# A row gather with three direct batches instead of five, a first index group of two, and slots dealt from another table

## The chip, the cores and the metric

The kernel runs on one core of a Trainium2 chip. The metric is the device time of one execution in microseconds (us); the median over several executions is compared. The engines of the core run side by side, each through its own list of instructions in order: TensorE (PE, with PEld for its weight loads), VectorE (DVE), ScalarE (ACT), GpSimd (POOL) and SyncE (SP). Transfers between memory and the chip run on sixteen DMA engines that all queues share.

## The reference

There are 32 batches. Each has a table of 512 rows with 1024 float32 values, and 128 row numbers; the output of a batch is the rows that the numbers name, in their order.

```python
batch, seq, dim = 32, 512, 1024
x = np.random.randn(batch, seq, dim).astype(np.float32)
indices = np.random.randint(0, seq, (batch, 128)).astype(np.int32)
...
for b in range(batch):
    result[b] = x[b, indices[b]]
```

Row numbers repeat within a batch. In the inputs of this case a batch names between 110 and 120 different rows, so about one row in nine or ten would be read twice by a plain gather. All 4096 output rows of 4 KB (16.8 MB) have to be written.

## The kernel before, in words

**Direct batches.** The first `HEAD` = 5 batches are gathered plainly: GpSimd issues an indirect DMA of 128 rows into a block (line 144, through `gather`, line 121), and SyncE stores the block (`store`, line 137). They need only the row numbers as a column, which `idxT` (line 112) holds after one transpose on TensorE; batch 0 has its column from a small load of its own.

**Packed batches.** The other 27 batches read each different row once. They stand in groups of three (`GROUP`), and for each group the index work has three steps. `step0` (line 166) spreads the row numbers of each batch over all partitions (`bc`, by TensorE), counts for every position how many earlier positions name the same row (`junk`, `cnt`, on VectorE), and marks the first of each kind as its leader (`lead`); `past` adds up the leaders of earlier batches. `step1` (line 183) numbers the leaders (`rk`, `nth`), and compares these numbers with the table `turn` (line 92), which says for each of the 128 slots which number it takes (`pack`). `step2` (line 196) puts the leader's row number into its slot (`pos`, `at`), with a value over the limit in the empty ones, and makes the matrix `s` that says which output row is served by which slot. `fetch` (line 207) issues the indirect DMA into one of `RING` = 8 buffers `u`; a slot with a value over the limit moves nothing. `spread_rows` (line 238) multiplies `s` with the buffer on TensorE (two halves of 512 columns), ScalarE copies the result from PSUM into the block, and SyncE stores it.

A number runs on from batch to batch (through `past`, taken modulo 128), so the empty slots of the next batch begin where those of the last one ended. `turn` comes from `rank`, eight GpSimd iotas (lines 73 to 79).

**The half batch.** Batch `HALF` = `HEAD` is served in two ways. Its rows below 256 are loaded plainly and early by ScalarE's queue (`early`, line 101) and spread by `half_rows` (line 225) with `last` false, four TensorE instructions for each half of the columns; only its rows from 256 on are gathered. `half_spread` (line 217) makes the matrix `same` for this on VectorE.

**Order.** TensorE, VectorE and ScalarE's first instructions run in the order in which the program names them (`InOrder`, line 13); GpSimd and SyncE too. Ahead of the main loop four groups (`AHEAD`) are prepared (lines 249 to 262). As buffers are eight, gathers up to batch `HEAD + RING - 1` = 12 are issued there. In this stretch `half_rows` for the first half stands after group 1's steps, and for the second half after group 2's. The main loop (line 263) takes the batches in turn: spread it, store it, fetch the batch eight further on into the buffer that came free, and do one of the three steps for the group four further on.

PSUM holds two buffers of `bc` (line 58), so that of a group is written anew two groups later, after all its readers.

Of the kernel before, what the change touches and what calls it, by code (L numbers as in the profile page):

```python
# [6 lines left out]
F32 = mybir.dt.float32  # L7
# [21 lines left out]
def kernel(ctx, tc, x, indices, out):  # L29
# [11 lines left out]

    nc = tc.nc
    B, S, D = x.shape
    N = indices.shape[1]
    HEAD, RING, GROUP, AHEAD, FAR = 5, 8, 3, 4, 1024
    HALF = HEAD
    PAIRED = range(12, 20)
    GROUPS = (B - HEAD) // GROUP  # L50
    assert 2 * N <= S <= FAR and (B - HEAD) % GROUP == 0
    const = ctx.enter_context(tc.tile_pool(name="const", bufs=1))
    ring = ctx.enter_context(tc.tile_pool(name="ring", bufs=1))
    rows = ctx.enter_context(tc.tile_pool(name="rows", bufs=1))
# [15 lines left out]

    diff = const.tile([N, N], I32, name="diff")
    nc.gpsimd.iota(diff[:], pattern=[[1, N]], base=0, channel_multiplier=-1)
    rank = const.tile([N, 8, 16], I32, name="rank")
    for e in range(8):
        fold = 0
        for bit, col in enumerate((6, 5, 3)):
            fold ^= col * (e >> bit & 1)
        steps = [[(-16 if fold >> bit & 1 else 16) << bit, 2] for bit in (2, 1, 0)]
        nc.gpsimd.iota(rank[:, e], pattern=[[1, 2]] + steps, base=2 * e + 16 * fold, channel_multiplier=0)
    less = const.tile([N, 1], F32, name="less")  # L80
    zero = const.tile([N, 1], F32, name="zero")
    dve(v.memset, zero[:], 0.0)
# [6 lines left out]
    dve(v.tensor_copy, out=less[:], in_=diff[:, 0:1])  # L89
    every = const.tile([N, N], F16, name="every")  # L90
    dve(v.memset, every[:], 1.0)
    turn = const.tile([N, N], F16, name="turn")
    dve(v.tensor_copy, out=turn[:], in_=rank[:].rearrange("p e q -> p (e q)"))
    vf = const.tile([N, N], F16, name="vf")
    dve(v.memset, vf[:], 0.0)
    dve(v.tensor_copy, out=vf[:B],
        in_=vals[:].bitcast(I32).rearrange("p (n two) -> p n two", two=2)[:, :, 0])


    xf = x.flatten_outer_dims()  # L100
# [49 lines left out]

    cnt, lead, slot = table("cnt", F32), table("lead", F16), table("slot", F16)
    nth, at = table("nth", I32), table("at", I32)
    past = const.tile([N, B + 1], F16, name="past")
    dve(v.memset, past[:, HEAD:HEAD + 1], 0.0)
    bcs, packs, spread = {}, {}, {}

    def of_group(g):
        return range(HEAD + g * GROUP, HEAD + (g + 1) * GROUP)

    def cols(t, g):  # L160
        return t[:, HEAD + g * GROUP:HEAD + (g + 1) * GROUP]

    def wide(t):
        return t.rearrange("p (g o) -> p g o", o=1).to_broadcast([N, GROUP, N])

    def step0(g):

        bcs[g] = bc = pbc.tile([N, 4, N], F32, name="bc")
        for k, b in enumerate(of_group(g)):
            pe(mm, bc[:, k], lhsT=ident[:, b:b + 1].to_broadcast([N, N]), rhs=vf[:], start=True, stop=True)  # L170
        for k, b in enumerate(of_group(g)):
            junk = junkp.tile([N, N], F16, name="junk")
            dve(v.scalar_tensor_tensor, out=junk[:], in0=bc[:, k], scalar=idxF[:, b:b + 1], in1=below[:],
                op0=ALU.is_equal, op1=ALU.mult, accum_out=cnt[:, b:b + 1])
        if HALF in of_group(g):
            c = slice(HALF, HALF + 1)
            dve(v.scalar_tensor_tensor, out=cnt[:, c], in0=idxF[:, c], scalar=2.0 * N, in1=cnt[:, c],
                op0=ALU.is_lt, op1=ALU.add)
        dve(v.tensor_scalar, out=cols(lead, g), in0=cols(cnt, g), scalar1=0.0, scalar2=None, op0=ALU.is_equal)
        for b in of_group(g):  # L180
            dve(v.tensor_tensor, out=past[:, b + 1:b + 2], in0=past[:, b:b + 1], in1=lead[:, b:b + 1], op=ALU.add)

    def step1(g):

        rk = psm.tile([N, GROUP], F32, name="rk")
        pe(mm, rk[:], lhsT=above[:], rhs=cols(lead, g), start=True, stop=False)
        pe(mm, rk[:], lhsT=every[:], rhs=cols(past, g), start=False, stop=True)
        dve(v.tensor_copy, out=cols(nth, g), in_=rk[:])
        dve(v.tensor_scalar, out=cols(nth, g), in0=cols(nth, g), scalar1=N - 1, scalar2=None, op0=ALU.bitwise_and)
        dve(v.scalar_tensor_tensor, out=cols(slot, g), in0=cols(cnt, g), scalar=256.0, in1=cols(nth, g),  # L190
            op0=ALU.mult, op1=ALU.add)
        packs[g] = pack = junkp.tile([N, GROUP, N], F16, name="pack")
        dve(v.tensor_tensor, out=pack[:], in0=turn[:].rearrange("p (o n) -> p o n", o=1).to_broadcast([N, GROUP, N]),
            in1=wide(cols(slot, g)), op=ALU.is_equal)

    def step2(g):

        pos = psm.tile([N, GROUP], F32, name="pos")
        for k, b in enumerate(of_group(g)):
            pe(mm, pos[:, k:k + 1], lhsT=packs[g][:, k], rhs=near[:, b:b + 1], start=True, stop=True)  # L200
        dve(v.tensor_scalar, out=cols(at, g), in0=pos[:], scalar1=float(FAR), scalar2=None, op0=ALU.add)
        s = pick.tile([N, GROUP, N], F32, name=f"s{g}")
        dve(v.tensor_tensor, out=s[:], in0=bcs[g][:, :GROUP], in1=wide(cols(at, g)), op=ALU.is_equal)
        for k, b in enumerate(of_group(g)):
            spread[b] = s[:, k]

    def fetch(b):
        if HEAD <= b < B:
            gather(held[(b - HEAD) % RING][:], at[:, b:b + 1], b, bounds_check=S - 1, oob_is_err=False)
# [7 lines left out]
    def half_spread():  # L217

        same = pick.tile([N, 2, N], F32, name="same")
        for k in range(2):  # L220
            dve(v.tensor_scalar, out=same[:, k], in0=bcs[0][:, HALF - HEAD], scalar1=less[:], scalar2=float(k * N),
                op0=ALU.add, op1=ALU.is_equal)
        spread[HALF, "early"] = [same[:, k] for k in range(2)]

    def half_rows(h, last):
        w = slice(h * 512, (h + 1) * 512)
        if not last:
            spread[HALF, h] = pout.tile([N, 512], F32, name="ps")
        ps = spread[HALF, h]
        if last:  # L230
            pe(mm, ps[:], lhsT=spread[HALF], rhs=held[(HALF - HEAD) % RING][:, w], start=False, stop=True)
        else:
            for k in range(2):
                pe(mm, ps[:], lhsT=spread[HALF, "early"][k], rhs=early[k][:, w], start=k == 0, stop=False)
        if last:
            nc.scalar.copy(out=blocks[HALF][:, w], in_=ps[:])  # L236
# [10 lines left out]
        store(b)  # L247

    step0(0)
    step0(1)  # L250
    for g in range(AHEAD):
        step1(g)
        if 0 < g < AHEAD - 1:
            step0(g + 1)
        step2(g)
        for b in of_group(g):
            if b < HEAD + RING:
                fetch(b)
        if g == 0:
            half_spread()  # L260
        elif g < 3:
            half_rows(g - 1, False)
    for b in range(HEAD, B):
        spread_rows(b)
        fetch(b + RING)
        g, step = divmod(b - HEAD, GROUP)
        if g + AHEAD < GROUPS:
            (step0, step1, step2)[step](g + AHEAD)


# [28 lines left out]
```

## Time and profile before

| | us |
|---|---|
| median of 9 runs | 88.13 |
| range of the runs | 87.92 to 89.08 |
| the profiled execution, its own time | 88.75 |
| its span, first to last instruction | 87.0 |

| engine | busy us | share of the span |
|---|---|---|
| TensorE | 62.2 | 72% |
| ScalarE | 40.6 | 47% |
| GpSimd | 33.5 | 39% |
| VectorE | 31.6 | 36% |

The transfers of the profiled execution are 32.91 MB, 379 GB/s over the span. The queue q1 carries the stores and the loads of the row numbers (SyncE), q0 the gathers (GpSimd), q10 the two early loads (ScalarE).

How to read the lines of a profile: in the order of time a line has its start in us, how long it took (for merged instructions: from the first start to the last end, or their sum), the engine, the line of the program, the operation, the tiles written and read, and the number of instructions; in brackets stands how long the engine was idle before and what ended that. "issue" is idle time for which the trace shows no wait. A line number can be that of a helper: the instructions that go through `InOrder` show line 21 or 24, those of both gathers line 122.

### The profile page before, as it was taken

What the parts mean: (1) busy time and instruction counts of PE and PEld (TensorE: products, weight loads), DVE (VectorE), ACT (ScalarE), POOL (GpSimd) and SP (SyncE); (2) the same over time, 40 slices, a digit from 0 to 9 for tenths busy, and PEclk for the clock granted to TensorE, in tenths of its full rate; (3) what the DMA queues carried; (4) which work ended last, traced back from release to release, by engine and by line L of the source; (5) the groups of instructions that cost most, each with busy time, mean ns of one, the idle gap of its engine ahead of it and who ended that gap; (6) DMA issues with size and microseconds to landing.
All of it is one profiled execution on the core that took longest, in us unless ns stands there. A gap on an engine that the chain in (4) does not pass through costs nothing.

```text
span 87.0 us, 829 instructions
## 1 busy us (share of the span) xinstructions
PE 62.2 (72%) x189; PEld 25.5 (29%) x189; DVE 31.6 (36%) x160; ACT 40.6 (47%) x63; POOL 33.5 (39%) x45
## 2 busy tenths in 40 slices
PE   0040169596799999999999988778878888785000
PEld 0030133241344444443544443222333333221000
DVE  3289895582565386473754850000000000000000
ACT  0999910000165665566566555553454454555000
POOL 7557577738044455554445554333400000000000
PEclk9999999999999999999999999999999999999955
DMA  0898999999999999999999999999999999999950
GB/s 1 279 403 237 290 317 394 416 411 416 420 418 420 420 416 420 420 416 409 420 420 420 413 418 418 422 422 415 420 415 415 420 418 422 418 422 420 420 243 11
DMA packets 9637, 32.91 MB, mean 379 GB/s; under 512 B 1585, under 2 KB 1617, under 8 KB 9633
## 3 DMA queue, kind: packets, MB, share of 16 engines
q1 hardware_dynamic: 4736, 16.81, 47.5%
q0 software_dynamic: 4608, 15.01, 44.6%
q10 hardware_dynamic: 288, 1.05, 3.2%
q8 instruction: 1, 0.02, 0.1%
q14 instruction: 4, 0.02, 0.1%
HBM read 17.86 MB, written 16.78 MB: 398 GB/s over the span
## 4 chain that ended last, share of the span: by engine, by line
DMA 37%; PE 30%; DVE 11%; issue 11%; POOL 2%; ACT 1%; SPq 0%; POOLq 0%; DVEq 0%
DMA u<-in_x_dram,at 34%; PE ps L24 27%; DMA vals<-in_indices_dram 3%; DVE pack L24 3%; DVE junk L24 2%; DVE nth L24 2%; POOL u L122 2%; DVE past L24 1%; PE pos L24 1%; DVE slot L24 1%; ACT block L246 1%; DVE s L24 1%; DVE same L24 1%; PE bc L24 1%; SPq L66 0%
## 5 line engine op out<-in xcount | busy, mean ns | idle before, releaser
L24 PE MATMUL ps<-u,s 128*128 128x512 f32 x108 | 52.0, 610 | 5.0 <-DMA u<-in_x_dram,at 5.0
L122 POOL DMA_INDIRECT u<-in_x_dram,at x27 | 26.9, 997 | 25.3 <-PE bc L24 6.3
L246 ACT COPY block<-ps 128x512 f32<-128x512 f32 x36 | 21.1, 586 | 18.8 <-PE ps L24 17.8
L24 PEld LDWEIGHTS ps<-u,s 128*128 128x128 f32 x108 | 18.3, 189 | 26.8 <-ACT block L246 15.0
L246 ACT COPY pair<-ps 128x512 f32<-128x512 f32 x16 | 9.4, 586 | 5.8 <-PE ps L24 4.2
L24 DVE SCALAR_TENSOR_TENSOR junk<-bc,idxF,below 128x128 f16<-128x128 f32 x27 | 8.0, 348 | 6.2 <-PE bc L24 6.2
L24 ACT COPY u<-zero 128x1024 f32<-128x1024 f32 x8 | 7.7, 1038 | 0.0
L24 PE MATMUL ps<-early,same 128*128 128x512 f32 x8 | 7.5, 1092 | 0.0
L236 ACT COPY block<-ps 128x512 f32<-128x512 f32 x2 | 1.2, 586 | 12.7 <-PE ps L24 12.7
L24 PE MATMUL pos<-near,pack 128*128 128x1 f16 x27 | 2.0, 167 | 5.5 <-DVE pack L24 5.5
L24 DVE TENSOR_TENSOR pack<-turn,slot 128x384 f16<-128x384 f16 x9 | 5.0, 558 | 0.3
L24 DVE TENSOR_TENSOR s<-bc,at 128x384 f32<-128x384 f32 x9 | 5.0, 558 | 0.3
L24 DVE TENSOR_TENSOR past<-past,lead 128x1 f16<-128x1 f16 x27 | 4.4, 163 | 0.9
L122 POOL DMA_INDIRECT block<-in_x_dram,idxT x4 | 3.8, 947 | 2.0 <-DVE past L24 1.0
L24 PEld LDWEIGHTS <-pack 128*128 128x128 f16 x27 | 1.7, 100 | 9.5 <-DVE pack L24 8.0
L24 PE MATMUL bc<-vf,ident 128*128 128x128 f16 x27 | 3.4, 256 | 1.3 <-DVE same L24 1.3
L24 PEld LDWEIGHTS <-ident 128*128 128x128 f16 x27 | 2.4, 112 | 4.2 <-issue 4.2
L21 PE MATMUL pos<-ident,vf 128*128 128x32 f16 x1 | 0.2, 209 | 4.2 <-DVE vf L24 4.2
L24 PEld LDWEIGHTS ps<-early,same 128*128 128x128 f32 x8 | 2.4, 324 | 2.1 <-issue 2.1
L24 DVE TENSOR_SCALAR at<-pos 128x3 int32<-128x3 f32 x9 | 1.4, 160 | 4.2 <-PE pos L24 3.8
L24 DVE CAST nth<-rk 128x3 int32<-128x3 f32 x9 | 1.4, 160 | 4.2 <-PE rk L24 3.5
L24 ACT ACT_TABLE_LOAD x1 | 1.3, 1283 | 2.2 <-DVE ident L24 2.2
(31 smaller groups left out, 18.0 us busy)
## 6 DMA issues: line engine op xcount, KB each, us to landing
out_dram<-block SPq DMA_DIRECT2D x24, 512.0 KB, 8.3
out_dram<-pair SPq DMA_DIRECT2D x4, 1024.0 KB, 12.5
early<-in_x_dram ACTq DMA_DIRECT2D x2, 512.0 KB, 4.2
u<-in_x_dram,at POOLq DMA_INDIRECT x27, 11.6
block<-in_x_dram,idxT POOLq DMA_INDIRECT x4, 7.0
vals<-in_indices_dram SPq DMA_DIRECT2D x1, 32.0 KB, 2.7
first<-in_indices_dram SPq DMA_DIRECT2D x1, 1.0 KB, 1.8
block<-in_x_dram,first POOLq DMA_INDIRECT x1, 5.0
```

The lines of the kernel that those rows point to most:

```text
L21: self.last = do(*args, **kw)
L24: self.last = do(*args, **kw)
L122: nc.gpsimd.indirect_dma_start(out=dst, out_offset=None, in_=xf[:], in_offset=bass.IndirectOffsetOnAxis(ap=at, axis=0), element_offset=b * ...
L236: nc.scalar.copy(out=blocks[HALF][:, w], in_=ps[:])
L246: nc.scalar.copy(out=blocks[b][:, w], in_=ps[:])
```

## The change

- `HEAD` is 3 instead of 5: batches 3 and 4 are packed, 29 in all, and the half batch is 3. The eight buffers now take batches 3 to 10 ahead of the loop.
- The groups are lists: the first has two batches (3 and 4), the nine others three.
- The steps are cut into smaller functions. `step0` is `spread_indices` (TensorE) and `find_leads` (VectorE); `step2` is `fill_slots` (to `at`) and `match` (`s`). In the stretch ahead of the loop, the next group's `spread_indices` stands before `fill_slots`, its `find_leads` after it, and `match` last. `half_spread` moves from the end of group 0 to a place behind `step1` of group 1, and the two calls of `half_rows` come one group later: after `fill_slots` of groups 2 and 3.
- Numbers in a group come from accumulated matmuls (`earlier`): each batch adds the leaders of the batches before it in its group; `past` is kept once a group, in `count_on`, behind `match`.
- The table `turn` has two parts. The first deals sixteen consecutive numbers to the slot groups (4 slots each) in another order; group 0 reads it from PSUM, where a matmul spreads it. The second part is for the last two batches (`APART`), which start from number 0 each; it puts their last numbers, which stay empty, into slots 38, 39, 42, 43, 46, 47, 50, 51, 71 to 76 and 104.
- The cast of `turn` on VectorE moves behind that of `vf`.
- In the main loop each group of batches does the three steps for the group four further on; the first group has two batches, so two of the steps stand after its second batch.

```diff
-    HEAD, RING, GROUP, AHEAD, FAR = 5, 8, 3, 4, 1024
+    HEAD, RING, GROUP, AHEAD, FAR = 3, 8, 3, 4, 1024
...
-    GROUPS = (B - HEAD) // GROUP
+    APART = B - 2
+    groups = [range(HEAD, HEAD + 2), *(range(b, b + GROUP) for b in range(HEAD + 2, B, GROUP))]
...
-    rank = const.tile([N, 8, 16], I32, name="rank")
-    for e in range(8):
-        fold = 0
-        for bit, col in enumerate((6, 5, 3)):
-            fold ^= col * (e >> bit & 1)
-        steps = [[(-16 if fold >> bit & 1 else 16) << bit, 2] for bit in (2, 1, 0)]
-        nc.gpsimd.iota(rank[:, e], pattern=[[1, 2]] + steps, base=2 * e + 16 * fold, channel_multiplier=0)
+    rank = const.tile([N, 2, N], I32, name="rank")
+    nc.gpsimd.iota(rank[:, 0], pattern=[[8, 2], [64, 2], [1, 8], [16, 4]], base=0, channel_multiplier=0)
+    for p0, p1, at0 in ((0, 38, 0), (52, 71, 44), (77, 104, 63), (105, N, 90), (71, 77, 121), (104, 105, 127)):
+        nc.gpsimd.iota(rank[:, 1, p0:p1], pattern=[[1, p1 - p0]], base=at0, channel_multiplier=0)
+    twos = rank[:, 1, 38:54].rearrange("p (k a l) -> p k a l", a=2, l=2)
+    nc.gpsimd.iota(twos[:, :3, 1], pattern=[[2, 3], [1, 2]], base=38, channel_multiplier=0)
+    nc.gpsimd.iota(twos[:, :, 0], pattern=[[2, 4], [1, 2]], base=113, channel_multiplier=0)
...
-    turn = const.tile([N, N], F16, name="turn")
-    dve(v.tensor_copy, out=turn[:], in_=rank[:].rearrange("p e q -> p (e q)"))
...
+    turn = const.tile([N, 2, N], F16, name="turn")
+    dve(v.tensor_copy, out=turn[:], in_=rank[:])
...
+        if g == 0:
+            pe(mm, bc[:, GROUP], lhsT=ident[:, 0:1].to_broadcast([N, N]), rhs=turn[:, 0], start=True, stop=True)
...
     def step1(g):
 
         rk = psm.tile([N, GROUP], F32, name="rk")
-        pe(mm, rk[:], lhsT=above[:], rhs=cols(lead, g), start=True, stop=False)
-        pe(mm, rk[:], lhsT=every[:], rhs=cols(past, g), start=False, stop=True)
-        dve(v.tensor_copy, out=cols(nth, g), in_=rk[:])
+        n, like = len(groups[g]), dealt_on(g)
+        earlier = [(k, lead[:, groups[g][0]:groups[g][0] + like - k]) for k in range(1, like)]
+        if g:
+            earlier.append((0, past[:, g:g + 1].to_broadcast([N, like])))
+        pe(mm, rk[:, :n], lhsT=above[:], rhs=cols(lead, g), start=True, stop=not earlier)
+        for i, (k, more) in enumerate(earlier):
+            pe(mm, rk[:, k:like], lhsT=every[:], rhs=more, start=False, stop=i == len(earlier) - 1)
+        dve(v.tensor_copy, out=cols(nth, g), in_=rk[:, :n])
...
+        table = turn[:, 0:1] if g else bcs[0][:, GROUP:]
+        dve(v.tensor_tensor, out=pack[:, :like], in0=table.to_broadcast([N, like, N]),
+            in1=wide(cols(slot, g)[:, :like], like), op=ALU.is_equal)
+        if like < n:
+            dve(v.tensor_tensor, out=pack[:, like:], in0=turn[:, 1:2].to_broadcast([N, n - like, N]),
+                in1=wide(cols(slot, g)[:, like:], n - like), op=ALU.is_equal)
...
     step0(0)
-    step0(1)
     for g in range(AHEAD):
         step1(g)
-        if 0 < g < AHEAD - 1:
-            step0(g + 1)
-        step2(g)
-        for b in of_group(g):
+        if g == 1:
+            half_spread()
+        if g < AHEAD - 1:
+            spread_indices(g + 1)
+        fill_slots(g)
+        for b in groups[g]:
             if b < HEAD + RING:
                 fetch(b)
-        if g == 0:
-            half_spread()
-        elif g < 3:
-            half_rows(g - 1, False)
-    for b in range(HEAD, B):
-        spread_rows(b)
-        fetch(b + RING)
-        g, step = divmod(b - HEAD, GROUP)
-        if g + AHEAD < GROUPS:
-            (step0, step1, step2)[step](g + AHEAD)
+        if g > 1:
+            half_rows(g - 2, False)
+        if g < AHEAD - 1:
+            find_leads(g + 1)
+        match(g)
+    for g, batches in enumerate(groups):
+        steps = [(step0, g + AHEAD), (step1, g + AHEAD), (step2, g + AHEAD)]
+        for b in batches:
+            spread_rows(b)
+            fetch(b + RING)
+            for step, ahead in steps if b == batches[-1] else steps[:1]:
+                if ahead < len(groups):
+                    step(ahead)
+            steps = steps[1:]
```

## The prediction

> **What bounds the kernel now.** I read the page first, part 2 and part 3.
>
> ```profile
> DMA  0898999999999999999999999999999999999950
> GB/s 1 279 403 237 290 317 394 416 411 416 420 418 420 420 416 420 420 416 409 420 420 420 413 418 418 422 422 415 420 415 415 420 418 422 418 422 420 420 243 11
> DMA packets 9637, 32.91 MB, mean 379 GB/s; under 512 B 1585, under 2 KB 1617, under 8 KB 9633
> ...
> q1 hardware_dynamic: 4736, 16.81, 47.5%
> q0 software_dynamic: 4608, 15.01, 44.6%
> ```
>
> A slice is 2.17 us. From slice 7 (15 us) to slice 37 the transfer engines run at 409 to 422 GB/s: 32.91 MB set the end, and what counts is whether the transfer queues ever run empty. The busy times by stage confirm the rate (columns: stretch, length, then busy us of PE, PEld, DVE, ACT, POOL, the clock, DMA share, GB/s).
>
> ```profile
> 24.00:28.00 4.00, 4.00 (x14) 1.72 (x13) 2.62 (x14) 2.53 (x5) 1.99 (x2) 1.00 1.03 417
> 28.00:84.00 56.00, 46.52 (x132) 18.43 (x130) 14.06 (x66) 28.72 (x49) 16.94 (x17) 0.99 1.02 417
> ```
>
> Next, the DMA view cut at 24 us and at 28 us (one line of each) says how much had been moved, and the view of 24 to 28 us what moved then.
>
> ```profile
> DMA packets 2437, 7.83 MB, mean 326 GB/s; under 512 B 502, under 2 KB 534, under 8 KB 2436
> ...
> DMA packets 2952, 9.50 MB, mean 339 GB/s; under 512 B 610, under 2 KB 642, under 8 KB 2951
> ...
> q0 software_dynamic: 486, 1.60, 98.6%
> q1 hardware_dynamic: 29, 0.07, 4.2%
> ```
>
> Between 24 and 28 us almost only gathers (q0) run: the early stores are used up and the first spread block isn't stored yet. The backlog of gathers, built before the main loop, keeps the engines busy there. Last, the order of time shows when that loop starts.
>
> ```profile
> 2.77 1.12 POOL L122 DMA_INDIRECT block<-in_x_dram,first  x1 [0.46 <-DMA first<-in_indices_dram]
> ...
> 8.69 0.94 POOL L122 DMA_INDIRECT block<-in_x_dram,idxT  x1 [0.30 <-issue]
> ...
> 9.64 0.16 DVE L24 TENSOR_SCALAR at<-pos 128x3 int32<-128x3 f32 x1 [0.34 <-PE rk L24]
> ...
> 10.59 1.00 POOL L122 DMA_INDIRECT u<-in_x_dram,at  x1 [0.96 <-ACT u L24]
> ...
> 12.13 3.76 PE L24 MATMUL ps<-early,same 128*128 128x512 f32 x4
> ...
> 17.32 3.73 PE L24 MATMUL ps<-early,same 128*128 128x512 f32 x4
> ...
> 20.90 0.99 POOL L122 DMA_INDIRECT u<-in_x_dram,at  x1 [0.30 <-issue]
> ...
> 22.45 1.96 PE L24 MATMUL ps<-u,s 128*128 128x512 f32 x4
> ...
> 24.69 1.00 POOL L122 DMA_INDIRECT u<-in_x_dram,at  x1 [2.80 <-PE bc L24]
> ```
>
> The gather at 20.90 is the eighth and last that the ring's eight buffers allow. The ninth waits until TensorE has read the first buffer: the loop starts at 22.45 and that gather goes out at 24.69.
>
> **The margin before.** What is queued ahead of the loop: early rows 1.05 MB, five direct gathers plus eight packed ones (640 + 864 rows of 4 KB, counting the distinct indices of the inputs) 6.16 MB, five stores 2.62 MB; together 9.83 MB. With 9.50 MB moved by 28 us it lasts to 28.8. The gather of 24.69 has its first packet some 2.3 us later (the first gather, issued at 2.77, has its first packet record at 5.08), at 27.0. So the engines stay fed by 1.8 us.
>
> **What the skill says.** "DMA: Bandwidth & Descriptors", section Issuing engines are not separate DMA queues: transfers of ScalarE, SyncE and GpSimd share the same sixteen engines and interleave. The trace agrees: q0 and q1 together stay at 417 GB/s whichever leads. The same page, The descriptor swizzle: the engine of partition p is 8*(p>>6) + ((p>>2)&7). No view names an engine; the count below rests on this. "TensorE: Matmul & The Clock Gate", Part 1: a cold array runs at half clock until a free-running window of about 3.4 us was busy throughout. The trace agrees: the fp32 matmuls of the 12.13 and 17.32 rows start 0.85 us apart, those of 22.45 0.43 us; the change came at 20.9 us.
>
> **The change, part by part.**
>
> *Two direct batches become packed (HEAD 5 to 3).* Removed: two direct gathers of 128 rows, 0.94 us and a 0.30 us gap each on POOL. Added: two packed ones (56 rows for the half batch 3, 111 for batch 4), two pairs of spread matmuls (1.9 us each), four copies (0.59 each). By count 3664 gathered rows become 3632: 0.13 MB less, 0.3 us at 417 GB/s. The matmuls and copies lie under the transfers of the loop (46.5 of 56 us are PE's there). But the queue ahead of the loop shrinks: early 1.05, gathers 384 + 852 rows 5.06, three stores 1.57: 7.68 MB instead of 9.83. Before moved 7.83 MB by 24 us, so this is gone at 23.7, and the ninth gather would have to be issued by 21.4.
>
> *When does the loop start?* Followed by rows of before.
> - Iotas on POOL: eight of 16 elements took 1.26 us; nine now, the largest 128 elements (like diff, 0.22): about 1.45. They end near 2.5; the gather waits to 2.77 for its indices anyway. Cost 0 to 0.1; past the cover it would delay the first gather one for one.
> - The cast of turn (256 columns, about 0.36 by the 128-column row's 0.23) moves behind vf, 4.15 to 4.5; TensorE's transpose lies beside it until 4.44. Cost 0 to 0.05.
> - Group 0 (batches 3, 4): two junk instead of three saves 0.27; no second step0 and no past chain ahead of nth save 2.2 (before, lead ended at 6.05 and nth began at 8.15). nth 6.0, then 0.2 each to slot, pack of 256 elements from PSUM 0.43 (a new form: 384 fp16 took 0.56, 384 fp32 from PSUM 0.56, so 0.35 to 0.56), pos 0.25, at done near 7.45 (before 9.80). The gather followed at by 0.79; so 8.25. POOL would be free at 7.44.
> - Group 1: three junk and lead 1.1, s of two 0.43, past 0.35, nth to pack 1.2 to 10.7, same 0.55 (half_spread now stands ahead of fill_slots), then bc of group 2, which waits for same (before too: PE bc <- DVE same 1.3), pos, at near 12.0; gathers 12.8, 14.1, 15.4.
> - Group 2: junk to lead 1.1, s 0.56, past 0.6, nth to pack 1.2, hops 0.5: pos near 15.6; gathers 16.8, 18.1, 19.4. The last is batch 10, as 3 + 8 is 11.
> - Half rows: the first pair begins at 15.7 and holds TensorE 3.6 us cold (12.10 to 15.68 before). Group 3's rk, queued behind it, runs at 19.35; nth to pos takes 1.55 (15.7 to 17.2 before): 20.9. Only then the second pair, 3.6: **loop at 24.5, not 22.45.** Before, both pairs were over when group 3's chain ended; here the second comes after it, and batch 3's matmuls are queued behind.
> - Batch 3: 1.8 us warm, 3.6 cold. TensorE works without a break from 20.9; a busy window ends between 24.3 and 27.7. I take 2.6: 27.1. The ninth gather (0.44 later, as 24.25 to 24.69) goes at 27.5, its packets at 29.8. The store (0.8 later, as 24.25 to 25.07) goes at 27.9, its packets 1.0 to 2.5 later (a load on idle engines 1.0, store 0 2.5, from the packet records). **Transfers resume at about 29.2: idle for 5.5 us**, bounds 4.3 to 6.7.
>
> *Rest.* 32.78 - 7.68 = 25.1 MB at 417 GB/s are 60.2 us: 89.4. For before the same sum gives 28.0 + 23.41/0.417 = 84.1; the landing records of the last store have a mean of 84.37.
>
> *The first group's steps in the loop.* Step1 and step2 of group 4 both follow batch 4, so pos waits on TensorE for pack, 1.5 us, with batch 5's matmuls behind. The two batches before it supply 30.7 rows per engine, 4.8 us; batch 5 is done 5.5 us after batch 3. Cost 0 to 0.7; taken 0.5: 89.9. Later groups have one step per batch as now.
>
> *Dealing.* By the map both dealings give each engine the same total (229 rows each before; 227 after, if the last two batches were dealt alike). In the landing records of before's last store the engines end at 83.38 to 86.05: three stand out, 1.68, 1.07 and 0.56 beyond the mean. With the last two batches apart, engine 10 gets 219 rows, 2 to 4 get 225, engine 1 and 9 and 11 227, the others 228 or 229. At 0.157 us a row (65536 B at 417 GB/s) engine 10 is 1.26 us below the mean, the others at most 0.31 above. If the late engines are those, the last ends 0.75 beyond the mean: 0.9 gained. If not, up to 0.3 lost. Taken: 90.65.
>
> *The other edits* (count_on behind s, no past memset, accumulating matmuls of 0.03 to 0.17) are in the chains above; in the loop they hide under transfers, and cost 0.2 a group where that cover is gone.
>
> **Sum.** 90.65 and the 0.95 after the last landing (86.05 to 87.0): span 91.6, 4.6 over before. The profiled execution took 88.75, 0.62 over the median of 88.13; I put the difference on the median: **92.7 us**.
>
> **Rivals.**
> 1. *The gap is shorter (0.12).* TensorE is warm by the second half pair. It then takes 1.8 instead of 3.6 and batch 3 1.8: resuming at 26.8, 2.4 sooner, 90.3 us. For it: one window's phase decides. Against: before, the first pair did not warm the array.
> 2. *The gap and no relief (0.14).* The late engines are others than the table's: 0.9 lost again and 0.3 more, 93.9 us. The view can't tell.
> 3. *No gap, faster (0.05).* If the ninth gather is out by 21.4 us, the queues never empty; then only 0.3 (rows) and 0.9 (dealing) remain: 86.9 us. For it: group 0 is ready 2.3 us sooner. Against: two cold half pairs and group 3's chain fill 15.7 to 24.5 on TensorE.
> 4. *Nothing moves (0.02)*: a small gap of about 1 us against the dealing, 88.1.
>
> My forecast has 0.67, its own range 91.5 to 93.7. **Numbers.** The 8-in-10 range takes the cases of rivals 1 and 2 in part: 90.5 to 94.2. Under 0.5% this kernel's runs can't be told from no change; slower 0.93, same 0.02, faster 0.05.
>
> **What would show it.** Right: GB/s falls to near zero in slices 11 to 13, q0 and q1 both; the eighth packed gather is issued near 19.4 and the ninth near 27.5; the first "ps<-u,s" stands near 24.5, after the second "ps<-early,same"; at least 0.12 MB less in q0; the tail of lone packets after the mean is shorter. Wrong: the ninth gather before 22 us, or a GB/s line without a hole. A hole that starts later than 24 us means slower transfers at the start, which the sum doesn't need.

## The result, and the profile after

The kernel after the change takes 93.07 us (median of 10 runs, 91.33 to 94.3), the one before 88.13. The ratio is 1.039 (95% interval 1.035 to 1.044): slower by 3.5 to 4.4%. Ratios, here and below, are taken from the runs within 1.5% of each kernel's fastest alone, which for the kernel after are the three between 91.33 and 91.92 us; the medians are of all runs, and stand 5.6% apart here. The profiled execution took 94.18 us with a span of 91.9, against 88.75 and 87.0 before.

Parts 2 and 3 of the page of the kernel after (a slice is 2.30 us):

```profile
DMA  0899999999349999999999999999999999999940
GB/s 5 293 367 383 364 346 387 303 349 423 143 175 242 403 348 348 407 424 410 407 426 408 419 419 419 423 412 423 421 415 421 419 424 414 419 423 415 417 194 11
DMA packets 9636, 32.78 MB, mean 357 GB/s; under 512 B 1616, under 2 KB 1648, under 8 KB 9632
...
q1 hardware_dynamic: 4736, 16.81, 46.0%
q0 software_dynamic: 4608, 14.88, 42.7%
```

There is a hole in slices 10 to 12 (counted from 0; 23 to 30 us), where before stood 418 and 420 GB/s, and q0 has 0.13 MB less, as counted. The late slices are as fast as before. The busy times by stage put the loss into two stretches (columns as in the prediction: stretch, length, busy us of PE, PEld, DVE, ACT, POOL, clock, DMA share, GB/s):

```profile
23.00:26.50 3.50, 3.50 (x12) 1.56 (x11) 1.07 (x7) 1.52 (x3) 1.00 (x1) 1.00 0.23 94
26.50:37.00 10.50, 9.23 (x40) 4.19 (x38) 6.12 (x30) 5.51 (x10) 4.61 (x5) 1.00 0.98 340
37.00:84.00 47.00, 42.93 (x126) 17.15 (x124) 11.98 (x58) 26.34 (x45) 15.31 (x16) 1.00 1.03 418
```

The first is the hole: 3.5 us at 94 GB/s lose 2.7 us of work at 418. The second is the restart: the engines count as busy (0.98) but move only 340 GB/s, which loses another 2.0 us over 10.5 us. From 37 us on the rate is the one before. The DMA view cut at 24 and at 28 us:

```profile
DMA packets 2466, 7.65 MB, mean 319 GB/s; under 512 B 576, under 2 KB 608, under 8 KB 2465
...
DMA packets 2620, 8.23 MB, mean 294 GB/s; under 512 B 588, under 2 KB 620, under 8 KB 2619
```

Before it was 7.83 and 9.50 MB. At 24 us nearly all of the 7.68 MB that the prediction counted ahead of the loop was gone. By 40 us the two stand at 12.54 and 14.53 MB, 2.0 MB apart: 4.8 us at 418 GB/s. The order of time says what the queue waited for:

```profile
6.76 0.16 DVE L24 TENSOR_SCALAR at<-pos 128x2 int32<-128x2 f32 x1 [0.31 <-PE pos L24]
...
14.75 3.76 PE L24 MATMUL ps<-early,same 128*128 128x512 f32 x4
...
18.52 1.00 POOL L126 DMA_INDIRECT u<-in_x_dram,at  x1 [0.30 <-issue]
...
19.95 3.37 PE L24 MATMUL ps<-early,same 128*128 128x512 f32 x4
...
23.15 1.88 PE L24 MATMUL ps<-u,s 128*128 128x512 f32 x4
...
25.31 1.00 POOL L126 DMA_INDIRECT u<-in_x_dram,at  x1 [5.79 <-PE bc L24]
```

The row of 18.52 is the eighth packed gather, that of 25.31 the ninth. Between them GpSimd waits 5.79 us for a buffer, and the buffer for the loop's first batch, which TensorE starts at 23.15 after two pairs of half rows. (The bracket names `bc` because those matmuls follow in TensorE's list; the ones that read the buffer run from 23.15 to 25.03. The gather's row numbers had been ready since 20.3.) Before, the loop started at 22.45, only 0.7 us sooner, but with 2.15 MB more in the queues.

Where the span's 4.9 us are: the sixteen engines finish the last store on average at 88.84 us instead of 84.37 (4.5 us), and the last engine comes 2.16 us after that mean instead of 1.68 (0.5 us). What follows the last landing is unchanged (0.9 us).

### The profile page after: what moved, and what is told of

It reads as the page before. It is cut to its first block, busy times and chain, and to the rows that moved or that the text cites. A ratio compares the mean times of both kernels' runs of the same rounds, so it can differ in the third digit from the quotient of the medians.

```text
span 91.9 us, 911 instructions
## 1 busy us (share of the span) xinstructions
PE 65.8 (72%) x220; PEld 28.0 (30%) x220; DVE 33.4 (36%) x170; ACT 42.9 (47%) x67; POOL 33.7 (37%) x46
## 4 chain that ended last, share of the span: by engine, by line
PE 43%; DMA 20%; DVE 12%; issue 8%; POOL 6%; ACT 1%; POOLq 1%; SPq 0%; DVEq 0%
PE ps L24 39%; DMA u<-in_x_dram,at 18%; POOL u L126 6%; DVE pack L24 3%; DVE junk L24 2%; DMA vals<-in_indices_dram 2%; DVE nth L24 2%; PE bc L24 2%; PE pos L24 1%; PE rk L24 1%; DVE slot L24 1%; DVE s L24 1%; DVE past L24 1%; DVE lead L24 1%; ACT block L286 1%
## 5 line engine op out<-in xcount | busy, mean ns | idle before, releaser
L24 PE MATMUL ps<-u,s 128*128 128x512 f32 x116 | 55.3, 609 | 4.1 <-DMA u<-in_x_dram,at 3.4
L126 POOL DMA_INDIRECT u<-in_x_dram,at x29 | 28.9, 997 | 30.8 <-PE bc L24 11.7
L286 ACT COPY block<-ps 128x512 f32<-128x512 f32 x40 | 23.4, 585 | 20.4 <-PE ps L24 19.0
L24 PEld LDWEIGHTS ps<-u,s 128*128 128x128 f32 x116 | 20.0, 191 | 26.9 <-issue 14.2
L276 ACT COPY block<-ps 128x512 f32<-128x512 f32 x2 | 1.2, 586 | 13.0 <-PE ps L24 13.0
L24 DVE TENSOR_TENSOR s<-bc,at 128x384 f32<-128x384 f32 (+1 forms) x10 | 5.4, 541 | 0.2
L24 DVE TENSOR_TENSOR pack<-turn,slot 128x384 f16<-128x384 f16 (+2 forms) x10 | 5.1, 518 | 0.3
L24 PE MATMUL rk<-lead,above 128*128 128x3 f16 (+1 forms) x10 | 1.8, 176 | 3.7 <-DVE lead L24 3.7
L24 DVE CAST nth<-rk 128x3 int32<-128x3 f32 (+1 forms) x10 | 1.6, 161 | 6.8 <-PE rk L24 6.8
L24 DVE TENSOR_SCALAR at<-pos 128x3 int32<-128x3 f32 (+1 forms) x10 | 1.6, 162 | 5.4 <-PE pos L24 5.4
L24 PEld LDWEIGHTS <-every 128*128 128x128 f16 x26 | 1.5, 102 | 3.9 <-issue 3.9
```

Of the source, the lines that this page charges most:

```text
L24: self.last = do(*args, **kw)
L126: nc.gpsimd.indirect_dma_start(out=dst, out_offset=None, in_=xf[:], in_offset=bass.IndirectOffsetOnAxis(ap=at, axis=0), element_offset=b * ...
L286: nc.scalar.copy(out=blocks[b][:, w], in_=ps[:])
```

## The experiments

My theory: the loop's first read of a buffer comes after the queues ran dry, because of two things at once: less work is queued (three direct batches), and the half rows come one group later. Its rivals: one of the two does it alone, or the loss lies elsewhere, in TensorE's added matmuls or in the dealing. Each kernel differs from the kernel after, if not said otherwise; the short names e1 to e12 are used below. The kernel before was timed again beside them, at medians of 88.2 to 88.4 us, and the ratios are to these runs. "Lateness" below is how far the last engine lands behind the mean of the sixteen in the last store.

**e1: one table.** The last two batches are dealt like the others.

```diff
-    APART = B - 2
+    APART = B
```

> The changed kernel, with the last two batches dealt like all others (APART = B), so no table of their own. Theory G (the queues run dry ahead of the main loop) expects the hole in the transfers at 23 to 26.5 us to stay, the time within 0.6 us of the changed kernel's 91.3 to 94.3, and the last engine of the last store 0.2 to 0.4 us nearer to the mean of the sixteen than the 2.16 us there, since the table gives the unlisted engines 16 rows in two batches instead of 14.2. Rival S (the table of the last two batches made the late engines later and is the main loss) expects 88 to 89.5 us.

Measured: 92.53 us (91.26 to 93.41). The profile has the same hole (loop at 21.72, ninth gather at 23.87), and a lateness of 1.67 us. So the separate dealing of the last two batches neither makes the loss nor, in this kernel, gains anything that shows.

**e2: five direct batches, everything else new.**

```diff
-    HEAD, RING, GROUP, AHEAD, FAR = 3, 8, 3, 4, 1024
+    HEAD, RING, GROUP, AHEAD, FAR = 5, 8, 3, 4, 1024
-    groups = [range(HEAD, HEAD + 2), *(range(b, b + GROUP) for b in range(HEAD + 2, B, GROUP))]
+    groups = [range(b, b + GROUP) for b in range(HEAD, B, GROUP)]
```

> The changed kernel with HEAD = 5 again and nine groups of three; new order, new tables and cut steps stay. G expects no hole (GB/s over 400 in every slice from 15 us to the tail), 9.83 MB queued ahead of the loop, and 87.5 to 88.9 us. Rival S expects 91 to 93, since the table stays. Rival M (the split steps and their order make the main loop slower) expects 90 to 93 too.

Measured: 90.6 us (90.34 to 91.39), ratio to before 1.033 (1.023 to 1.043). I was wrong: the hole is only later. Order of time, then the stage, of this kernel:

```profile
22.08 3.76 PE L24 MATMUL ps<-early,same 128*128 128x512 f32 x4
...
25.64 2.78 PE L24 MATMUL ps<-u,s 128*128 128x512 f32 x4
...
28.68 1.00 POOL L126 DMA_INDIRECT u<-in_x_dram,at  x1 [7.04 <-PE bc L24]
```

```profile
28.00:32.00 4.00, 4.00 (x16) 1.74 (x15) 2.13 (x11) 2.50 (x5) 2.00 (x2) 1.00 0.59 180
```

With 9.83 MB queued the supply lasts to about 28 us, as in the kernel before, but the half rows now end after 25.6 and the ninth gather goes out at 28.68, four microseconds later than before's 24.69. The late half rows alone are enough for a hole. That the queue was shortened, which the prediction put first, isn't needed for it. The loop starts later here than in the kernel after (25.64 against 23.15), whose first group has only two batches; so this shows what the late half rows do with five direct batches, and not how much of the loss they make in the change itself.

**e3: half rows early, three direct batches.**

```diff
-        if g > 1:
-            half_rows(g - 2, False)
+        if 0 < g < 3:
+            half_rows(g - 1, False)
```

> The changed kernel with the two halves of the early rows one group sooner again (after groups 1 and 2), so that the second lies ahead of group 3's chain. G expects the loop's first matmul near 21.4 us instead of 23.15, the ninth gather as much sooner, the hole 1.5 to 2 us shorter and the time 1.0 to 2.0 us lower than the changed kernel on this chip. S and M expect no change (within 0.4).

Measured: 91.2 us (90.43 to 92.41), ratio 1.034 (1.024 to 1.045). Loop at 22.41, a microsecond later than I expected, and ninth gather at 24.65, as before the change, and still a dip to 260 GB/s. So the shorter queue alone is enough too.

**e5: both undone, five direct batches and early half rows.** The edits of the last two together; the new steps, the accumulated counts and both tables stay.

> The changed kernel with HEAD = 5, groups of three, and the two halves of the early rows one group sooner: both causes of theory G undone, while the new tables, the cut steps and the new order of the index work stay. G expects no hole, the loop near 22.4 us and 87.6 to 88.8 us. Rival R (the remaining edits cost by themselves, as the 90.6 us of the five-direct run may mean) expects 90 to 91 us. The run with five direct batches alone, 90.6 us, had its loop at 25.64 us and a hole at 28 to 31 us; G takes that late loop for the whole of its loss.

Measured: 87.27 us (86.76 to 88.45, 6 runs), ratio 0.987 (0.979 to 0.995). Page, order of time and stage of this kernel:

```profile
GB/s 1 235 381 290 275 269 420 414 414 418 420 418 418 420 416 420 418 420 414 414 418 420 414 423 418 418 420 422 420 416 416 425 418 416 418 423 420 418 410 84
```

```profile
22.56 1.96 PE L24 MATMUL ps<-u,s 128*128 128x512 f32 x4
...
24.80 0.99 POOL L126 DMA_INDIRECT u<-in_x_dram,at  x1 [4.04 <-PE bc L24]
```

```profile
28.00:84.00 56.00, 46.72 (x138) 18.49 (x136) 13.77 (x67) 28.81 (x50) 16.87 (x17) 0.99 1.03 418
```

From the seventh slice to the last but one none falls under 410. This version is faster than both kernels, than the one before by 0.5 to 2.1%, on six runs, and a little faster than I expected. The four corners are, in us:

| | half rows early | half rows one group later |
|---|---|---|
| five direct batches | 87.27 | 90.6 |
| three direct batches | 91.2 | 93.07 (a second set of runs: 92.08) |

Either edit alone costs 3.3 to 3.9 us, both 4.8 to 5.8 and not the sum of 7.3. The queue's length and the loop's start act on one margin (1.8 us before), and each edit alone already uses it up. The rows differ clearly, but in the lower one the two entries aren't clear of each other: with three direct batches the runs with early half rows lie between 90.43 and 92.41 us, those with late ones between 91.33 and 94.3.

**Where e5's gain comes from.** The mean landing of its last store is 84.57, no sooner than before's 84.37 and 84.54 (two profiles). What differs in these profiles is the tail. The DMA view over the last 7 us, cut in 40 slices of 0.17 us, of the kernel after (85 to 91.9 us) and of this one (78.8 to 85.8):

```profile
GB/s 427 475 404 380 451 404 404 404 451 404 427 428 380 380 404 380 380 332 261 119 119 95 71 71 71 24 24 24 24 24 47 24 0 0 0 0 0 0 0 0
```

```profile
GB/s 445 421 421 398 398 421 398 421 445 468 398 398 421 421 398 398 468 421 445 398 421 421 375 421 445 421 375 421 328 328 211 164 70 0 0 0 0 0 0 0
```

24 GB/s in such a slice is one packet of 4 KB: in the kernel after the last 1.2 us belong to a single engine. In e5 the engines end within 1.3 us of each other (83.68 to 85.00), and its lateness is 0.43 us. Two things could do this: the new tables, or the new order of the index work.

**e10: the tables alone, in the kernel before.** Both new tables, with what they need in the counting, and nothing else.

```diff
-    rank = const.tile([N, 8, 16], I32, name="rank")
...
+    rank = const.tile([N, 2, N], I32, name="rank")
...
-        dve(v.tensor_tensor, out=pack[:], in0=turn[:].rearrange("p (o n) -> p o n", o=1).to_broadcast([N, GROUP, N]),
-            in1=wide(cols(slot, g)), op=ALU.is_equal)
+        dve(v.tensor_tensor, out=pack[:, :like], in0=turn[:, 0:1].to_broadcast([N, like, N]),
+            in1=wide(cols(slot, g))[:, :like], op=ALU.is_equal)
+        if like < GROUP:
+            dve(v.tensor_tensor, out=pack[:, like:], in0=turn[:, 1:2].to_broadcast([N, GROUP - like, N]),
+                in1=wide(cols(slot, g))[:, like:], op=ALU.is_equal)
```

> The kernel before with the two dealing tables alone: five direct batches, old groups and order, but the empty slots of batches 30 and 31 at the listed places. Theory T (the table relieves the engines that end last, as long as the transfers never pause) expects 86.7 to 87.4 us, all sixteen engines within 0.6 us of their mean at the last store (1.68 and 1.63 in the two profiles of before), and the mean unchanged near 84.4. The rival (the gain of the version with five direct batches and early halves, 87.27 us, comes from the new order of the index work) expects 88.0 to 88.6.

Measured: 88.02 us (87.03 to 89.86, 13 runs), ratio 0.992 (0.989 to 0.996). The runs fall in two heaps, 87.0 to 88.0 and 88.8 to 89.9. Only three of the 13 lie where I expected all, the median lies in the rival's range, and the ratio rests on the better heap alone; over all runs the gain on the kernel before is 0.3 us (88.36 to 88.02). The profiled execution (span 85.2) is the fastest of all. In it the last engine lands 0.6 us behind the mean, as the tables should do, but the mean itself came 0.7 us sooner too (83.69). So the tables may shorten the tail; that they make e5's gain isn't shown.

**e8: the kernel before once more**, for the spread of its profile.

> The kernel before once more, for a second profile: whether the engine that ends last in the last store is again 1.7 us beyond the mean of the sixteen, and whether the 16 KB instruction fetch (at 48.3 us, 0.945 us long) comes at the same place. If the late engines are the same in every execution, a table that names them can help; if the lateness differs by 0.5 us or more between executions, it can't be dealt with by a fixed table.

Measured: 88.34 us (20 runs), ratio 1.002 (0.9995 to 1.004); lateness 1.63 us, as in the first profile (1.68). The late engine of the kernel before is no accident of one profile. The 16 KB instruction fetch did not come at the same place: it stands at 42.98 us here, at 48.3 in the first profile.

**e9: the best version with one table.** e5 with `APART = B`.

> Five direct batches, early halves, the new order of the index work, but the last two batches dealt like the others (APART = B). T expects 88.0 to 88.7 us and the last engine 1.4 to 1.9 us beyond the mean at the last store. The rival (order of the index work) expects 87.0 to 87.5.

Measured: 89.39 us (87.27 to 90.22, 6 runs). The profiled execution doesn't answer the question, since another thing happened in it. Clock line of the page, and order of time:

```profile
PEclk9999999955556999999999999999999999999755
```

```profile
24.33 3.76 PE L24 MATMUL ps<-u,s 128*128 128x512 f32 x4
...
28.36 1.00 POOL L126 DMA_INDIRECT u<-in_x_dram,at  x1 [5.83 <-PE bc L24]
```

From 17.6 to about 28 us the clock was granted at 0.5 to 0.6. The second half pair and the loop's first batch took 3.76 us each, and the ninth gather went out 3.6 us later than in e5: a hole, with not one instruction of this stretch changed. The last engine lands 0.95 us behind the mean, less than the 1.4 that I expected at least, but after a hole; and one run, at 87.27 us, is as fast as e5's median. On the table this run is inconclusive, and if anything against my theory; on the margin it shows that a slow array of some 10 us uses it up.

**e4: more buffers.** Ten instead of eight, and the fetch behind the index steps so that it finds its row numbers.

```diff
-    HEAD, RING, GROUP, AHEAD, FAR = 3, 8, 3, 4, 1024
+    HEAD, RING, GROUP, AHEAD, FAR = 3, 10, 3, 4, 1024
...
             spread_rows(b)
-            fetch(b + RING)
             for step, ahead in steps if b == batches[-1] else steps[:1]:
                 if ahead < len(groups):
                     step(ahead)
+            fetch(b + RING)
```

> The changed kernel with ten gather buffers instead of eight (and the fetch behind the index steps of its batch, which ten need). Batches 11 and 12 are gathered ahead of the loop, 236 rows or 0.97 MB more, 2.3 us of transfers. The loop starts no sooner. G expects the hole nearly closed (at most 1 us) and the time 2 to 4 us lower, 89 to 91. If instead the late start of the loop costs by itself (TensorE as the bound), the time stays within 0.5 us of the changed kernel's. S expects no change.

Measured: 91.67 us (90.25 to 92.76), ratio 1.033 (1.018 to 1.048), above the 89 to 91 that I expected. Two more gathers went out at 21.53 and 22.83 and the hole got smaller, but the second gather of the loop came only at 30.07, waiting for the row numbers of the fifth group: a second stall took the place of the first. Of the loss of the kernel after at most a third came back.

**e6: half rows inside the loop.** Three direct batches; batches 4 and 5 are spread ahead of the loop, and the half rows after batches 7 and 8, with batch 3 behind them. The cut parts start group 4's index steps ahead of the loop and put each fetch behind a step.

```diff
-        if g > 1:
-            half_rows(g - 2, False)
+        if g == 2:
+            spread_rows(4)
+        if g == 3:
+            fetch(12)
+            spread_rows(5)
...
+    for b in sorted([HALF, *range(6, B)], key=lambda b: b + 5.5 if b % RING == HALF else b):
+        if b == HALF:
+            half_rows(1, False)
+        spread_rows(b)
...
+        if b == 7:
+            half_rows(0, False)
```

> The changed kernel, three direct batches, with the half batch spread later: ahead of the loop TensorE spreads batch 4 (where the first half of the early rows stood) and batch 5 (where the second stood), and their buffers take batches 12 and 13 at once; the early rows are multiplied in the loop, after batches 7 and 8, and the half batch follows. Same bytes, same matmuls. G expects the ninth gather at 20 to 21.5 us, no hole over 0.5 us, and 87.3 to 88.6 us, up to 0.3 us under the kernel before for 0.13 MB less. Rival R expects 90 us or more. Rival M (TensorE's work in the loop as the bound) expects 89.5 or more, as the loop has 7 us more of it.

Measured: 92.81 us (92.21 to 94.29), ratio 1.050 (1.041 to 1.060): wrong by 4 us. Order of time and stage:

```profile
17.58 3.42 PE L24 MATMUL ps<-u,s 128*128 128x512 f32 x4 [2.60 <-DMA u<-in_x_dram,at]
...
23.03 0.99 POOL L126 DMA_INDIRECT u<-in_x_dram,at  x1 [3.40 <-DVE at L24]
```

```profile
28.00:46.00 18.00, 18.00 (x63) 8.00 (x63) 8.58 (x44) 8.96 (x16) 7.95 (x8) 1.00 0.96 342
```

The same stretch of the kernel before:

```profile
28.00:46.00 18.00, 18.00 (x66) 8.18 (x65) 10.57 (x50) 11.14 (x19) 9.38 (x10) 1.00 1.03 418
```

TensorE first waits 2.60 us for batch 4's rows. From 28 to 46 us it then works 18.00 of 18.00 us, while the transfers get 342 GB/s. In the kernel before it had no pause there either, so that the half rows pushed into the loop find no free time, and the index steps and the buffers come later: from 20 to 48 us GpSimd's gathers wait 9.9 us for `at`, in four waits. I read this as TensorE being the bound here, as rival M has it. It is argued, since the fetches also moved behind the index steps. If it holds, the time ahead of the loop isn't spare: half rows moved out of it come back in the loop.

**e11: TensorE kept busy.** The kernel of e3 (three direct, half rows early) with 14 added matmuls whose result nobody reads, in places where TensorE waits, so that the array comes up to its clock sooner.

```diff
+    def keep_busy(n):
+        ps = pout.tile([N, 512], F32, name="ps")
+        for _ in range(n):
+            pe(mm, ps[:].rearrange("p (a n) -> p a n", a=4), lhsT=every[:],
+               rhs=every[:].rearrange("p (o n) -> p o n", o=1).to_broadcast([N, 4, N]), start=True, stop=True)
...
         if g == 1:
+            keep_busy(4)
             half_spread()
...
+        if g != 1:
+            keep_busy(2)
         fill_slots(g)
...
+        if g == 0:
+            keep_busy(4)
```

> Three direct batches, early halves, and 14 matmuls of ones without a use (4 of 512 columns after group 0's slots, 4 after group 1's numbers, 2 in each other group's wait for pack), all where TensorE waited for VectorE anyway; they are there to bring the array's clock up before the half rows. Bytes, queues and buffers as in the changed kernel. Theory G expects: if the clock is up by 12 us, each pair of half rows takes 1.9 instead of 3.7 us, the loop's first matmul stands at 18.5 to 20, the ninth gather at 20.8 to 22.3 (21.4 is the point where the queue still reaches), the hole under 1 us, and the time 86.7 to 88.3 us. If the clock doesn't come up sooner, 90 to 91.5 as with early halves alone. A rival by which three direct batches cost 3 us for another reason than the loop's start (more packed batches, slower gathers) expects 90 or more with the loop at 19 too.

Measured: 88.89 us (87.87 to 90.55, 22 runs), ratio 1.003 (1.000 to 1.006), half a microsecond above what I expected. Order of time and stage:

```profile
12.02 1.96 PE L24 MATMUL ps<-early,same 128*128 128x512 f32 x4
...
19.71 1.96 PE L24 MATMUL ps<-u,s 128*128 128x512 f32 x4
...
21.95 0.99 POOL L126 DMA_INDIRECT u<-in_x_dram,at  x1 [1.31 <-PE bc L24]
```

```profile
24.00:28.00 4.00, 3.04 (x13) 1.52 (x14) 2.72 (x13) 1.41 (x3) 1.59 (x2) 1.00 1.02 412
```

The half pairs take 1.96 us instead of 3.76, the loop starts 2.7 us sooner than in e3, the hole is gone (412 GB/s from 24 to 28 us), and 2.3 us come back, with three direct batches and added work. This is the direct test of the mechanism: only what TensorE does ahead of the loop was changed, and no byte of the loads, gathers and stores.

**e12: the same with five direct batches.**

> Five direct batches, early halves and the same 14 matmuls. G expects nothing from a sooner loop where the transfers were fed already: 86.7 to 87.7 us, as the 87.27 us of the same kernel without them, with less spread. If the loop's start cost by itself, it would gain 2 us more.

Measured: 88.72 us (87.28 to 90.06, 22 runs), ratio 0.998 (0.994 to 1.002): no gain over before, and one microsecond more than I expected. The loop starts at 20.61, but there was no hole left to close. By 80 us it had moved 31.31 MB, e5 31.18; what it lost against e5 is mostly the tail, a lateness of 1.53 against 0.43 us. With both tables and no hole the tail is nearly as long as in the kernel before. In this profile a 16 KB instruction fetch of 0.965 us stands at 80.77, where e5's only one stands at 40.91; it may be what makes one engine late, but no view names the engine. With e11 this pair says that three direct batches cost nothing clear once the loop starts in time (88.89 against 88.72).

**e7: the kernel after once more.**

> The changed kernel once more, unaltered, for a second profile beside the others on the same chip. Theory G (the transfers run dry ahead of the main loop, by a smaller queue AND a later loop) expects again 117.2 rows per engine moved and then a hole, with the loop's first matmul between 21.7 and 25 us depending on when the array's clock comes up; 91.3 to 94 us.

Measured: 92.08 us (91.69 to 94.25), ratio 1.046 (1.037 to 1.054). In this profile the array came to its clock at 17.9 instead of 22.8 us: span 89.9, and in the order of time

```profile
21.37 1.88 PE L24 MATMUL ps<-u,s 128*128 128x512 f32 x4
...
23.52 0.99 POOL L126 DMA_INDIRECT u<-in_x_dram,at  x1 [4.26 <-PE bc L24]
```

The same program, 2 us apart, by the array's state in its first 25 us. And here the ninth gather goes out 1.2 us sooner than in the kernel before (24.69), and the hole is there all the same, with 255 GB/s from 24 to 28 us. In this execution the loop isn't late, and the shorter queue alone accounts for the hole.

**The ninth gather across runs.** Of the kernels with three direct batches and eight buffers, those that begin the loop with batch 3 stand in the same order by the ninth gather and by the time of the profiled execution, in us:

| | ninth gather | profiled execution |
|---|---|---|
| e11 | 21.95 | 89.22 |
| e7 | 23.52 | 91.69 |
| e1 | 23.87 | 92.15 |
| e3 | 24.65 | 92.41 |
| after | 25.31 | 94.18 |

The early half rows of e3 did not make its loop sooner than that of e7 or e1: its row numbers landed later (`vf` cast at 4.34, in e7 at 3.07) and both of its half pairs took the full 3.76 us. What the later half rows add to the loss, where the queue is short already, these runs don't show.

## Why the prediction was right, and where not

The time (92.7 against 93.07) and the mechanism, queues that run dry before the ninth gather, were right. That the time came so close is in part luck: the sizes of several steps were wrong, and their errors cancelled. Steps in their order:

- **The queue ahead of the loop** (7.68 MB, gone at 23.7 us): right. 7.65 MB had moved by 24 us.
- **What the packed gathers save** (0.13 MB): right to the digit.
- **The first group** (`at` near 7.45, eighth gather near 19.4): 0.7 to 0.9 too late. The row numbers landed sooner in this execution (`vf` cast at 3.23, before 3.95).
- **The loop's start** (24.5): measured 23.15. Of the 1.35 us, 0.95 were won by the start of the second half pair (19.95; I had 20.9), some 0.7 of them by the earlier row numbers; the other 0.4 is the clock, which came up inside this pair (3.37 instead of 3.76 us) and left batch 3 fully warm (1.88; I took 2.6). This is rival 1's mechanism in part. The ninth gather came at 25.31, not 27.5. In e7 and e1, which have the same program up to there, the loop starts at 21.37 and 21.72, sooner than before's 22.45. So the loop that comes later than before, which the prediction stressed, is seen in one execution of three.
- **The hole** (5.5 us idle, bounds 4.3 to 6.7): wrong, under the lower bound. It lost 2.7 us, and GB/s fell to 94 and not near zero for all of it. I had the transfers resume 1.7 us after the gather of 27.5; they resumed at 26.5, with the store, 1.2 after the gather of 25.31.
- **The remaining 25.1 MB at 417 GB/s**: wrong for the first third of it. I let the rate return at once and put 0.5 us on the first group's steps; the restart ran at 340 GB/s for 10.5 us and lost 2.0. Hole and restart together are 4.7 us, where I had 6.0: the two errors partly cancel. That the steps of group 4 delay batch 5 is there (its matmuls start at 28.42, 1.4 us after batch 4's end), but some packets of the stores and gathers after the hole are slow too (last section).
- **Mean landing of the last store** (89.9): 88.84, so 1.1 us sooner.
- **The dealing** (last engine 0.75 beyond the mean): wrong, and it was the outcome that I gave to rival 2. It is 2.16, and 1.91 in the second profile. What the tables do stays open. With both tables and no pause the lateness was 0.43 (e5), 0.6 (e10), 0.94 (e11) and 1.53 (e12), against 1.68 and 1.63 with the old table; these are single profiles, and the times of e10 and e12 show no clear gain. After a hole it was 1.2 to 2.2 with both tables, and 1.67 (e1) and 0.95 (e9) where the last two batches were dealt like the others. In the kernels with a hole and both tables the earliest engine ends 1.5 to 1.9 us ahead of the mean (after, e7, e2, e3, e4, e6); with a hole and `APART = B` it is 0.5 (e1, e9), without a hole 0.3 to 1.0. This fits an engine that catches up in the hole and is then relieved for nothing (the prediction gave engine 10 eight rows fewer, 1.26 us); it is argued, and no view names the engine.
- **Rival 3** (no gap, faster, 86.9): refuted for the change as made. e11 is the nearest test of it: the ninth gather is out at 21.95, the gap is gone, and the time is 88.89, not 86.9. The 87.27 us of e5 need five direct batches.

The errors add up to little: hole −2.8, restart +1.5, last engine +1.4, and the last landing came at 90.99 where I had 90.65. A total that close rests on three terms that were each off by more than a microsecond.

In the prediction I took the shorter queue as the cause and the later half rows as what makes it worse. The four corners say that each is sufficient, the late half rows with five direct batches (e2), the shorter queue with early half rows (e3); for the change as made, e7 puts the shorter queue first. The margin of 1.8 us read from the kernel before was the number that mattered: it stands against the 2.15 MB that left the queue, 5.2 us at 417 GB/s.

## What to carry to other kernels

Where transfers are the bound, work out the margin: how long what is queued lasts, against when the first instruction that frees a buffer can be done, and then price every edit ahead of the loop against this margin, not against the engines' busy shares. Edits that use up the same margin don't add up, so undo them one at a time and together before calling one harmless. Whether another dealing of the last batches pays isn't settled here: without a pause the last engine came anywhere from 0.43 to 1.53 us behind the mean.

## What the runs showed of the hardware

- **The rate stays low after a hole.** In the kernel after it was 340 GB/s for 10.5 us, so that a hole of 2.7 us of lost work cost another 2.0. In the packet records most packets of 4 KB took 0.159 us, as in steady flow. But those of the stores took about 0.30 from 27.4 to 28.1 us, and sixteen gather packets took over 0.5 us, up to 1.3, in two clusters (28.1 to 29.0 and 33.9 to 36.6 us). The kernel before and e5 have no such packet between 28 and 40 us. The second cluster comes more than 7 us after the transfers resumed, so what makes these packets slow is open. In e2 less was lost: 375 and 403 GB/s in the two stretches of 4 us after its hole.
- **The array's clock comes up at very different times for the same program**, here 22.8 and 17.9 us in two profiles of the kernel after; over all profiles, from 10.4 (e11, TensorE kept busy) to 27.4 (e2). "TensorE: Matmul & The Clock Gate", Part 1, of the Trainium skill speaks of a window of about 3.4 us that runs freely, whatever the kernel does. The runs agree that a busy array gets there (e11), but in most profiles a first pair of half rows, 3.76 us without a break, was not enough, and in e2 it took 5.3 us of unbroken matmuls (22.08 to 27.4); a free-running window that has to be busy for all or most of its length allows both. In e9 the rate fell back after 17.6 us. Only there does the page's clock line show a low rate while TensorE works; otherwise it stands at 9 from the start, and the rate must be read from the distance of the matmuls (0.85 or 0.43 us). Whether e9's fall and a cold array are the same thing is open.
- **The load of the row numbers** landed so that the `vf` cast began anywhere from 3.07 to 4.49 us, and the whole chain ahead of the loop moves with it.
